# A two-layer mixed-attention block on one core: Gram products and transposed operands of the recurrence in 64x64 tiles per head

## The chip, the cores and the metric

One core of one Trainium2 chip. The metric is the device time of one execution in microseconds (us). The kernel is timed three times and the median is taken.

## The reference

Two layers work on 1280 tokens (256 of context, 1024 latent) of width 1024. Each layer projects the modulated stream once and feeds three branches: A, a bidirectional linear recurrence (6 heads x 64); B, grouped-query attention (6 query heads); C, neighbourhood attention (4 heads). They are gated, joined, projected out and normalised.

```python
def _rwkv7_step(S, inp):
    r, w, k, v, kk, b = inp
    sa = jnp.einsum('bhvk,bhk->bhv', S, kk)
    S = S * w[:, :, None, :] - sa[..., None] * b[:, :, None, :] + v[..., None] * k[:, :, None, :]
    return S, jnp.einsum('bhvk,bhk->bhv', S, r)
...
def _layer(...):
    ...
    S_f, S_b, ys_c = _rwkv_bidir(rin_c, S0, S0)
    _, _, ys_l = _rwkv_bidir(rin_l, S_f, S_b)
    ...
    y_l = jnp.concatenate([yr_l * jax.nn.silu(rg_l), ya_l * jax.nn.silu(ag_l),
                           yn_l * jax.nn.silu(ng_l)], axis=-1) @ w_out
    x = _layer_norm(DEEPNORM_ALPHA * x + gate[:, None] * y_l, ln_g, ln_b)
```

Only branch A is touched by the change. It runs over the tokens forwards and backwards, from the context into the latents.

## The kernel before, in words

A layer has four parts in the program: the input projections (matmuls into `pj`, lines 203 to 205, and their evacuations), the recurrence (`rwkv`, line 516), the attention of branches B and C (`attention`, line 831), and the output projection with the norm (lines 1144 to 1312). The code is written part after part, but a list scheduler puts the instructions of each engine in order before the kernel is built: it takes whatever it holds to be ready, the code that stands first in the program ahead of the rest. So the last projections, the recurrence and the attention are interleaved on every engine. That order is fixed when the kernel is built. On the chip each engine works through its own queue in that order and waits at its head for semaphores.

The recurrence is chunked: 32 tokens are a chunk, 128 tokens a *wave*, so that a layer has ten waves (`NW`) in each direction. The three head pairs are `c`, the direction is `d`, and the head of a pair is `p`: its 64 channels lie on partitions 64p to 64p + 63. A wave has these stages:

- `wave_pre` (line 555): loads r, kk, kd and bd, makes the decay factors (tiles `psz`, `pcu`, `lp`, `iv`) and two operand tiles: `kb` (128 partitions x 3 x 4 x 64; for each chunk 32 columns of kd and 32 of bd) and `G`. `G` has for each head `p` a block of its own. The head's own 64 partitions get kk and r (GpSimd, lines 594 and 596); the other 64 partitions are filled with zeros (GpSimd, line 593).
- `wave_gram` (line 612): for each direction `d` and each half `h` of the four chunks, six matmuls (line 620) contract `kb` with `G` over all 128 partitions into the PSUM tile `gt`. The zeros keep the two heads of a pair apart. Chunk i of the half lands on partitions 64i on. Then four VectorE instructions (line 625) multiply by the triangular mask `msk` and write into that half of `G` which held the zeros. From there on a chunk of `G` is the whole operand of a step: kk and r of the head on one half, its Gram matrix on the other.
- `wave_low` (line 600) sends a part of `G` through DRAM (`ls_d`) into `lin`. `wave_inv` (line 641) inverts small triangles from it on VectorE (lines 644 to 659), and `wave_merge` (line 673) makes the tile `tt`.
- `wave_kt` (line 628): for each `d` and `h`, three transposes of 128x128 (line 635) turn `kb` into the PSUM tile `kt`, and four ScalarE copies (line 639) put its 64x64 blocks into `S`, where the identity stands already in the other half.
- `wave_chain` (line 692): the serial part. Four steps a wave, each a chain of matmuls into `ch` (lines 713, 724, 734) with a ScalarE copy (716), four copies into `X` (730) and two VectorE products with the decay (739) between them. `out_step` (748) reads the output into `py` and copies it to `yst` (756). GpSimd clears a part of each `X` (708).

The tiles `psz`, `pcu`, `gt`, `kt`, `mg`, `py` and `pso` share one PSUM pool with two buffers (`pa`, line 523). The outer loop (line 810) runs `wave_chain(w)`, then the stages i, k, m for wave w + 2 and p, g, l for wave w + 3. `G` has six buffers, so a wave's `G` is written again three waves later.

Attention works with `sm` (scores for the row maximum, line 894, read by VectorE at line 896), `st` (scores, lines 963 and 964, read by ScalarE at line 970) and `y` (values, line 948). It waits for nothing of the recurrence, and its rows fill the engines between the stages of the waves. What is left of it when the last wave is done is worked off alone, before the output projection. [...]

Of the kernel before, what the change touches and what calls it, by code (L numbers as in the profile page):

```python
# [8 lines left out]
F32 = mybir.dt.float32  # L9
F32R = mybir.dt.float32r  # L10
AF = mybir.ActivationFunctionType
ALU = mybir.AluOpType
# [31 lines left out]
def body(tc, a):  # L44
    nc = tc.nc
# [10 lines left out]
    ident = cload("ident", [128, 128], nc.gpsimd)  # L56
    bones = cload("bones", [128, 128], nc.gpsimd)
    pp = const.tile([128, DEPTH, NPC], F32, tag="pp", name="pp")
# [457 lines left out]
    def rwkv(l, lay):  # L516
# [6 lines left out]
        pa = es.enter_context(tc.tile_pool(name=f"pa{l}", bufs=2, space=PSUM))  # L523
# [6 lines left out]
        msk = rp.tile([128, 2, 64], F32, tag="msk", name="msk")  # L530
# [24 lines left out]
        def wave_pre(w):  # L555
            dc = r2.tile([128, 2, 4, 3], F32, tag="dc", name="dc", bufs=4)
            prep[w] = dict(dc=dc, d=[], g=[])
            for d in range(2):
                t0 = 128 * wave_block(w, d)
                need_r = not (last and t0 < TC)  # L560
# [24 lines left out]
                kb = r2.tile([128, 3, 4, 64], F32, tag="kb", name="kb", bufs=2)  # L585
# [3 lines left out]
                g = G[(2 * w + d) % 6]  # L589
                for p in range(2):  # L590
                    rs_ = slice(64 * p, 64 * p + 64)
                    gv = g[rs_, :, :, p, :].rearrange("q j c f -> q c j f")
                    nc.gpsimd.memset(g[64 - 64 * p:128 - 64 * p, :, :, p, 0:64 if need_r else 32], 0.0)
                    nc.gpsimd.tensor_tensor(out=gv[:, :, :, 0:32], in0=v4(ld["kk"])[rs_], in1=lp[rs_, :, :, d:d + 32], op=ALU.mult)
                    if need_r:
                        nc.gpsimd.tensor_tensor(out=gv[:, :, :, 32:64], in0=v4(ld["r"])[rs_], in1=lp[rs_, :, :, o:o + 32], op=ALU.mult)
# [15 lines left out]
        def wave_gram(w):  # L612
            for d in range(2):
                g, kb = prep[w]["g"][d], prep[w]["d"][d][0]
                nr = prep[w]["d"][d][1]
                for h in range(2):
                    gt = pa.tile([128, 3, 2, 64], F32, tag="pp", name="gt")
                    for c in range(3):
                        for i in range(2):
                            nc.tensor.matmul(out=gt[64 * i:64 * i + 64, c, :, :nr], lhsT=kb[:, c, 2 * h + i, :], rhs=g[:, 2 * h + i, c, :, :nr],  # L620
                                             start=True, stop=True, tile_position=(0, 64 * i))
                    for i in range(2):
                        rs_ = slice(64 * i, 64 * i + 64)
                        for p in range(2):
                            nc.vector.tensor_tensor(out=g[64 - 64 * p:128 - 64 * p, 2 * h + i, :, p, :nr], in0=gt[rs_, :, p, :nr],  # L625
                                                    in1=msk[rs_, d, :nr].unsqueeze(1).to_broadcast([64, 3, nr]), op=ALU.mult)

        def wave_kt(w):
            prep[w]["s"] = S[2 * w % 4:2 * w % 4 + 2]
            for d in range(2):  # L630
                g, kb = prep[w]["s"][d], prep[w]["d"][d][0]
                for h in range(2):
                    kt = pa.tile([128, 3, 128], F32, tag="pp", name="kt")
                    for c in range(3):
                        nc.tensor.transpose(kt[:, c, :], kb[:, c, 2 * h:2 * h + 2, :].rearrange("q j f -> q (j f)"), ident)
                    for p in range(2):
                        os_ = slice(64 - 64 * p, 128 - 64 * p)
                        for j in range(2):
                            nc.scalar.copy(g[os_, 2 * h + j, :, p, :], kt[64 * j:64 * j + 64, :, 64 * p:64 * p + 64])

        def wave_inv(w):

# [776 lines left out]
```

## Time and profile before

| what | value |
|---|---|
| time, median of 3 runs | 2471.63 us (2459.14 to 2474.3) |
| the profiled execution: time / span | 2478.63 us / 2476.9 us |
| TensorE / VectorE / GpSimd / ScalarE busy share | 88% / 66% / 48% / 41% |
| mean granted TensorE clock | 0.937 |
| the chain that ended last: TensorE / VectorE / DMA / issue / ScalarE / GpSimd | 44% / 21% / 15% / 7% / 6% / 4% |
| read-out copies of the chain steps (line 716), 40 a layer: first and last start | 410.5 to 2288.8 us |

How to read it. A group's row ends in "busy us, mean ns of one", and after the next bar stands the idle time of the engine just before these instructions with what ended it. A float32 matmul leaves two records, a transpose of line 635 one; so `gt` has 960 records for 480 matmuls and `kt` 240 for 240. A matmul's duration in a row is its latency: the next one on the array starts long before it ends. What a stream of them costs is the group's busy time over its count, or the length of a burst in the timeline. "issue" is time in which the engine waited for nothing that the profile shows. PEclk is the clock that TensorE was granted.

### The profile page before, as it was taken

Reading aid. Unit: us, or ns where it says so; the run is one execution under the profiler, and the core shown is the slowest. Engines: PE = TensorE matmul, PEld = TensorE weight load, DVE = VectorE, ACT = ScalarE, POOL = GpSimd, SP = SyncE. Lnnn points to the kernel's source line nnn. Section 1 sums busy time; section 2 is a strip of 40 time slices with the busy share of each in tenths; the row PEclk is TensorE's granted clock in tenths of the full one; section 3 lists DMA queues with packets and bytes.
Section 4 is the critical chain, followed back from the end, with each engine's and each line's share of the span. In section 5 each row is a group of like instructions: output and inputs, shape, how many; then the busy total and the mean of one; then the engine's idle time right before and its main releaser. Section 6 shows DMA issues by size and latency. Waiting matters only on the chain.

```text
span 2476.9 us, 57781 instructions
## 1 busy us (share of the span) xinstructions
PE 2189.6 (88%) x22616; PEld 1645.0 (66%) x22616; DVE 1625.1 (66%) x3063; ACT 1003.5 (41%) x2186; POOL 1184.1 (48%) x1438
## 2 busy tenths in 40 slices
PE   6989999987888888989899999899868788989697
PEld 3777898765555555545897777787645555556397
DVE  5686423545768777775396785525468688778646
ACT  3333413334445454463233434223345444445522
POOL 4464426335555554462245456434456545545433
PEclk9999999996879999998999999999879999999899
DMA  7344335446555444351332445334555545332522
GB/s 281 112 162 164 111 92 123 120 108 139 126 116 136 114 100 119 102 177 34 101 103 91 146 161 182 107 90 121 141 116 140 102 99 117 84 90 64 161 71 94
DMA packets 448241, 298.17 MB, mean 120 GB/s; under 512 B 249600, under 2 KB 395880, under 8 KB 446944
## 3 DMA queue, kind: packets, MB, share of 16 engines
q1 hardware_dynamic: 439936, 281.71, 41.6%
q0 software_dynamic: 7392, 10.28, 1.5%
q8 instruction: 178, 2.92, 0.5%
q10 hardware_dynamic: 640, 2.49, 0.4%
q14 instruction: 95, 0.78, 0.1%
HBM read 198.37 MB, written 91.79 MB: 117 GB/s over the span
## 4 chain that ended last, share of the span: by engine, by line
PE 44%; DVE 21%; DMA 15%; issue 7%; ACT 6%; POOL 4%; SPq 3%; DVEq 0%; POOLq 0%; ACTq 0%
PE pj L203 5%; PE pj L204 5%; PE pj L205 5%; PE y L948 4%; DMA yf<-yg_d 3%; PE st L963 3%; PE sm L894 3%; DMA ls_d<-G 3%; DVE G L625 2%; PE st L964 2%; DVE mx L896 2%; DVE tmp L653 2%; PE ch L734 2%; PE py L754 1%; DMA lin<-ls_d 1%
## 5 line engine op out<-in xcount | busy, mean ns | idle before, releaser
L204 PE MATMUL pj<-hlo,wh 128*128 128x512 f32 (+1 forms) x1072 | 401.4, 375 | 14.3 <-DVE hlo L480 8.0
L203 PE MATMUL pj<-hhi,wh 128*128 128x512 f32 (+1 forms) x1072 | 403.2, 378 | 9.4 <-ACT qr L348 5.2
L205 PE MATMUL pj<-hhi,wl 128*128 128x512 f32 (+1 forms) x1072 | 400.6, 374 | 0.2 <-POOL wl L169 0.2
L204 PEld LDWEIGHTS pj<-hlo,wh 128*128 128x128 f32 x1072 | 205.0, 191 | 56.2 <-DVE hlo L480 8.3
L203 PEld LDWEIGHTS pj<-hhi,wh 128*128 128x128 f32 x1072 | 204.4, 191 | 54.8 <-issue 6.8
L169 POOL TENSOR_TENSOR wl<-wf,wh 128x512 fp32r<-128x512 f32 x104 | 143.8, 1387 | 202.2 <-ACT wh L168 178.7
L896 DVE TENSOR_REDUCE mx<-sm 128x1 f32<-128x512 f32 (+1 forms) x372 | 198.8, 554 | 50.1 <-PE sm L894 47.6
L205 PEld LDWEIGHTS pj<-hhi,wl 128*128 128x128 f32 x1072 | 204.9, 191 | 38.4 <-issue 3.3
L970 ACT ACTIVATE pt<-st 128x512 f32<-128x512 f32 (+1 forms) x292 | 164.9, 583 | 130.1 <-PE st L964 122.8
L948 PE MATMUL y<-pt,v 128*64 128x256 f32 (+1 forms) x1392 | 211.5, 398 | 2.3 <-ACT pt L973 1.4
L894 PE MATMUL sm<-k,q 128*128 128x256 f32 (+2 forms) x436 | 166.1, 422 | 25.8 <-DVE mx L896 19.5
L963 PE MATMUL st<-q,k 128*128 128x512 f32 (+3 forms) x376 | 165.0, 444 | 21.1 <-DVE rc L1012 5.9
L1186 PE MATMUL pj<-yh,wh 128*128 128x256 f32 x576 | 160.2, 290 | 24.4 <-ACT yh L1160 23.1
L1187 PE MATMUL pj<-yl,wh 128*128 128x256 f32 x576 | 164.0, 288 | 0.8 <-POOL yl L1161 0.8
L1188 PE MATMUL pj<-yh,wl 128*128 128x256 f32 x576 | 162.2, 286 | 0.0
L977 POOL TENSOR_TENSOR acc<-acc,pt 128x512 f32<-128x512 f32 x80 | 106.4, 1330 | 102.7 <-ACT pt L970 101.4
L948 PEld LDWEIGHTS y<-pt,v 128*64 128x64 f32 x1392 | 94.0, 142 | 89.6 <-issue 58.0
L964 PE MATMUL st<-q,k 65*128 65x512 f32 (+3 forms) x376 | 146.7, 393 | 1.9 <-ACT q L908 1.2
L894 PEld LDWEIGHTS sm<-k,q 128*128 128x128 f32 x436 | 80.6, 201 | 89.8 <-DVE mx L896 37.0
L625 DVE TENSOR_TENSOR G<-gt,msk 64x192 f32<-64x192 f32 (+1 forms) x320 | 110.5, 345 | 39.7 <-PE gt L620 28.4
L708 POOL MEMSET X<- 32x192 f32 x320 | 81.2, 254 | 102.0 <-PE py L754 74.6
L1186 PEld LDWEIGHTS pj<-yh,wh 128*128 128x128 f32 x576 | 109.9, 196 | 26.0 <-ACT yh L1160 23.5
(276 smaller groups left out, 5104.5 us busy)
## 6 DMA issues: line engine op xcount, KB each, us to landing
wf<-win SPq DMA_DIRECT2D x104, 256.0 KB
wm<-wmod SPq DMA_DIRECT2D x32, 512.0 KB
yf<-yg_d SPq DMA_DIRECT2D x72, 128.0 KB
wt<-wm SPq DMA_DIRECT2D x8, 1024.0 KB
gate_d<-o SPq DMA_DIRECT2D x32, 256.0 KB
wf<-wout SPq DMA_DIRECT2D x16, 512.0 KB
ldkk<-rw_d SPq DMA_DIRECT2D x40, 192.0 KB
ldkd<-rw_d SPq DMA_DIRECT2D x40, 192.0 KB
```

The source lines that it names most:

```text
L203: nc.tensor.matmul(out=ps[:, :n], lhsT=wh, rhs=hhi[:, k, t0:t0 + n], start=(k == 0), stop=False)
L204: nc.tensor.matmul(out=ps[:, :n], lhsT=wh, rhs=hlo[:, k, t0:t0 + n], start=False, stop=False)
L205: nc.tensor.matmul(out=ps[:, :n], lhsT=wl, rhs=hhi[:, k, t0:t0 + n], start=False, stop=(k == KT - 1))
L894: nc.tensor.matmul(out=sp_[:, :o], lhsT=q[0][:, qc:qc + 128], rhs=k[0][:, c0:c0 + o], start=True, stop=True)
L896: nc.vector.tensor_reduce(out=mx[:, n_:n_ + 1], in_=sp_[:, :o], op=ALU.max, axis=AX.X)
L948: mm = nc.tensor.matmul(out=y[64 * i:64 * i + 64, a0:a1], lhsT=v[:, t, :], rhs=pt[:, p0:p0 + a1 - a0], start=start, stop=stop and at == le ...
L963: nc.tensor.matmul(out=o, lhsT=k[0][:, 128 * t:128 * t + 128], rhs=q[0][:, qa:qb], start=True, stop=False)
L964: mm = nc.tensor.matmul(out=o, lhsT=k[1][0:65, 128 * t:128 * t + 128], rhs=q[1][0:65, qa:qb], start=False, stop=True)
L970: nc.scalar.activation(out=pt[:, :w], in_=sp_[:, :w], func=AF.Exp)
L1186: nc.tensor.matmul(out=p_, lhsT=wh[m][:, k], rhs=yh, start=(x_ == 0), stop=False)
L1187: nc.tensor.matmul(out=p_, lhsT=wh[m][:, k], rhs=yl, start=False, stop=False)
L1188: nc.tensor.matmul(out=p_, lhsT=wl[m][:, k], rhs=yh, start=False, stop=(x_ == KT - 1))
```

## The change

1. The zeros of line 593 go: 2 a wave and direction, 80 in all.
2. `wave_gram` contracts over the 64 partitions of one head at a time. For each `d` and `h` there are twelve matmuls of 64x64 by up to 64 columns instead of six of 128x64 by up to 128. Head 0 takes the array's rows 0 to 63 and columns 64 to 127, head 1 the rows 64 to 127 and columns 0 to 63, by turns. Each result lands on the partitions where `G` wants it, with both chunks of the half beside each other, and two masks of 64x384 do what four of 64x192 did.
3. `wave_kt` does the same with the identity as the moving operand: twelve matmuls of 64x64 instead of three transposes of 128x128, and two copies of 64x384 instead of four of 64x192.

Counts over the kernel: mask instructions 320 to 160, copies 320 to 160, zero fills 80 to 0, `gt` matmuls 480 to 960, `kt` 240 transposes to 960 matmuls.

```diff
@@ -590,7 +590,6 @@
                     rs_ = slice(64 * p, 64 * p + 64)
                     gv = g[rs_, :, :, p, :].rearrange("q j c f -> q c j f")
-                    nc.gpsimd.memset(g[64 - 64 * p:128 - 64 * p, :, :, p, 0:64 if need_r else 32], 0.0)
@@ -614,29 +613,34 @@
                 for h in range(2):
-                    gt = pa.tile([128, 3, 2, 64], F32, tag="pp", name="gt")
-                    for c in range(3):
-                        for i in range(2):
-                            nc.tensor.matmul(out=gt[64 * i:64 * i + 64, c, :, :nr], lhsT=kb[:, c, 2 * h + i, :], rhs=g[:, 2 * h + i, c, :, :nr],
-                                             start=True, stop=True, tile_position=(0, 64 * i))
+                    gt = pa.tile([128, 2, 3, 64], F32, tag="pp", name="gt")
                     for i in range(2):
-                        rs_ = slice(64 * i, 64 * i + 64)
-                        for p in range(2):
-                            nc.vector.tensor_tensor(out=g[64 - 64 * p:128 - 64 * p, 2 * h + i, :, p, :nr], in0=gt[rs_, :, p, :nr],
-                                                    in1=msk[rs_, d, :nr].unsqueeze(1).to_broadcast([64, 3, nr]), op=ALU.mult)
+                        for c in range(3):
+                            for p in range(2):
+                                rs_, os_ = slice(64 * p, 64 * p + 64), slice(64 - 64 * p, 128 - 64 * p)
+                                nc.tensor.matmul(out=gt[os_, i, c, :nr], lhsT=kb[rs_, c, 2 * h + i, :], rhs=g[rs_, 2 * h + i, c, p, :nr],
+                                                 start=True, stop=True, tile_position=(64 * p, 64 - 64 * p))
+                    for p in range(2):
+                        os_ = slice(64 - 64 * p, 128 - 64 * p)
+                        nc.vector.tensor_tensor(out=g[os_, 2 * h:2 * h + 2, :, p, :nr], in0=gt[os_, :, :, :nr],
+                                                in1=msk[os_, d, :nr].unsqueeze(1).unsqueeze(1).to_broadcast([64, 2, 3, nr]), op=ALU.mult)
...
-                    kt = pa.tile([128, 3, 128], F32, tag="pp", name="kt")
-                    for c in range(3):
-                        nc.tensor.transpose(kt[:, c, :], kb[:, c, 2 * h:2 * h + 2, :].rearrange("q j f -> q (j f)"), ident)
+                    kt = pa.tile([128, 2, 3, 64], F32, tag="pp", name="kt")
+                    for i in range(2):
+                        for c in range(3):
+                            for p in range(2):
+                                rs_, os_ = slice(64 * p, 64 * p + 64), slice(64 - 64 * p, 128 - 64 * p)
+                                nc.tensor.matmul(out=kt[os_, i, c, :], lhsT=kb[rs_, c, 2 * h + i, :], rhs=ident[rs_, rs_],
+                                                 start=True, stop=True, tile_position=(64 * p, 64 - 64 * p))
                     for p in range(2):
                         os_ = slice(64 - 64 * p, 128 - 64 * p)
-                        for j in range(2):
-                            nc.scalar.copy(g[os_, 2 * h + j, :, p, :], kt[64 * j:64 * j + 64, :, 64 * p:64 * p + 64])
+                        nc.scalar.copy(g[os_, 2 * h:2 * h + 2, :, p, :], kt[os_])
```

Since the scheduler orders each engine anew, rows move far from the edited lines. Lines behind the edit have numbers higher by 4 in the changed kernel. Three places follow.

TensorE in the first wave of layer 0, where the transposed operand stands beside the projections (`pj`) and the first chain step (`ch`). Before:

```order
L203 MATMUL pj<-hhi,wh 128x512
L635 MATMUL kt<-c_ident,kb 128x128 x3
L204 MATMUL pj<-hlo,wh 128x512
L205 MATMUL pj<-hhi,wl 128x512
L713 MATMUL ch<-X_2966,G_2949 32x64
L635 MATMUL kt<-c_ident,kb 128x128 x3
L713 MATMUL ch<-X_2966,G_2949 32x64
```

And in the changed kernel:

```order
L203 MATMUL pj<-hhi,wh 128x512
L639 MATMUL kt<-c_ident,kb 64x64 x24
L717 MATMUL ch<-X_2966,G_2949 32x64 x2
L717 MATMUL ch<-X_2966,G_2948 32x64 x2
L717 MATMUL ch<-X_2966,G_2949 32x64 x2
L717 MATMUL ch<-X_2966,G_2948 32x64 x2
```

Two bursts of three transposes have become one row of 24 small matmuls, two halves `h` in one go, with no projection between them.

VectorE at the masks of a later wave of layer 0, between rows of attention (`nm`, `pt`, `am`, `sm`, `acc`) and the chain's update of `X`. Before:

```order
L587 TENSOR_TENSOR kb<-ldkd,iv 128x12x32
L625 TENSOR_TENSOR G_2948<-gt,msk 64x3x64 x4
L901 TENSOR_REDUCE nm<-mx 128x1
L972 TENSOR_TENSOR pt_10837<-st,bt 128x384
L108 COPY am<-pmod 128x256
L625 TENSOR_TENSOR G_2948<-gt,msk 64x3x64 x4
```

And in the changed kernel, at the same direction of the same wave:

```order
L976 TENSOR_TENSOR pt_10972<-st,bt 128x384
L587 TENSOR_TENSOR kb<-ldkd,iv 128x12x32
L626 TENSOR_TENSOR G_2948<-gt,msk 64x6x64 x2
L905 TENSOR_REDUCE nm<-mx 128x1
L626 TENSOR_TENSOR G_2948<-gt,msk 64x6x64 x2
```

Two rows of four masks have become two rows of two, and less attention stands between them.

TensorE at the end of layer 0's recurrence: the last chain matmuls (`ch` from `S`) and the attention before them. The numbers at the names count tiles in program order; the same tile has a number higher by 400 in the changed kernel (`silu_10769` and `silu_11169` are one tile). Before:

```order
L963 MATMUL st<-q_12214,k_12206 128x512
L964 MATMUL st<-q_12215,k_9979 128x512
L894 MATMUL sm<-k_12206,q_12616 128x256
L907 MATMUL mt<-c_ident,nm 1x128
L754 MATMUL py<-X_2966,G_2948 32x64
L799 MATMUL pso<-c_ident,yo 128x128 x3
L754 MATMUL py<-X_2966,G_2948 32x64
L754 MATMUL py<-X_2966,G_2949 32x64
L894 MATMUL sm<-k_12206,q_12616 128x256
L105 MATMUL pmod<-wm,silu_10769 32x256 x4
L734 MATMUL ch<-X_2966,S_2956 64x64 x6
L734 MATMUL ch<-X_2966,S_2957 64x64 x6
```

And in the changed kernel:

```order
L952 MATMUL y<-pt_12458,v 64x128
L898 MATMUL sm<-k_11455,q_12207 128x512
L1027 MATMUL tb<-c_ident,rb 128x128 x4
L105 MATMUL pmod<-wm,silu_11169 32x256 x4
L758 MATMUL py<-X_2966,G_2948 32x64
L803 MATMUL pso<-c_ident,yo 128x128 x3
L758 MATMUL py<-X_2966,G_2948 32x64
L758 MATMUL py<-X_2966,G_2949 32x64
L898 MATMUL sm<-k_11455,q_12207 128x256
L898 MATMUL sm<-k_11455,q_12207 128x512
L738 MATMUL ch<-X_2966,S_2956 64x64 x6
L738 MATMUL ch<-X_2966,S_2957 64x64 x6
```

When the recurrence ends, the kernel before is at the keys `k_12206`, the first group of branch B. The changed one is still at the key tile before it (`k_11455`, that is 11055), the last head of branch C. Counted over the whole order, 128 of layer 0's 368 `y` matmuls stand behind the last chain row before and 172 in the changed kernel; in layer 1 it is 52 and 88 of 328.

## The prediction

> **What bounds the kernel now.** I read the page first, for the engines and for the chain of work that ended last:
>
> ```profile
> span 2476.9 us, 57781 instructions
> PE 2189.6 (88%) x22616; PEld 1645.0 (66%) x22616; DVE 1625.1 (66%) x3063; ACT 1003.5 (41%) x2186; POOL 1184.1 (48%) x1438
> PE 44%; DVE 21%; DMA 15%; issue 7%; ACT 6%; POOL 4%; SPq 3%; DVEq 0%; POOLq 0%; ACTq 0%
> ```
>
> No engine is full, and no engine has the chain to itself: it changes hands all the time. TensorE (PE) has 44% of it and VectorE (DVE) 21%. So an instruction removed counts by the share of its kind that lies on the chain, not by its whole duration.
>
> The averages mix stages, so I read the windows next. The edited lines run while the waves run. I cut each layer into the stretch of steady waves (eight of the ten) and the tail behind the last wave, where attention is alone:
>
> ```profile
> core 0: us, PE busy (x) PEld busy (x) DVE busy (x) ACT busy (x) POOL busy (x), PEclk, DMA share, GB/s
> 600.00:1055.00 455.00, 395.76 (x6237) 261.02 (x6234) 345.86 (x886) 225.20 (x570) 242.36 (x332) 0.91 0.49 118
> 1055.00:1188.00 133.00, 120.03 (x774) 68.04 (x773) 86.23 (x160) 65.03 (x127) 55.46 (x40) 0.93 0.33 99
> 1840.00:2289.00 449.00, 393.80 (x6110) 253.12 (x6111) 366.86 (x882) 224.44 (x542) 245.73 (x329) 0.95 0.43 100
> 2289.00:2345.00 56.00, 44.56 (x315) 24.12 (x313) 44.56 (x67) 34.20 (x65) 28.82 (x19) 0.95 0.45 135
> ```
>
> In the waves PE is busy 87% and 88% of the time, DVE 76% and 82%, while ScalarE (ACT) and GpSimd (POOL) are half idle. Two engines close to full, each waiting for the other in the order of its queue: that is the bound, some 57 us a wave (455 over 8).
>
> How much of the chain are the edited lines? The chain of waits by line, once for 720 us around layer 0's recurrence and once for 670 us around layer 1's:
>
> ```profile
> by line: PE y L948 4.9%; issue 4.8%; PE pj L205 4.6%; PE pj L204 4.6%; PE pj L203 4.5%; DMA ls_d<-G 4.3%; DVE G L625 4.2%; DMA X<-vt_d 3.4%; PE st L963 3.3%; PE sm L894 3.1%; ACT S L639 2.5%; DVE tmp L653 2.4%; PE ch L734 2.3%; DVE e L655 2
> by line: PE y L948 6.8%; PE sm L894 5.3%; issue 5.2%; DMA ls_d<-G 5.0%; DVE G L625 4.0%; PE pj L205 3.9%; PE st L963 3.8%; PE pj L204 3.8%; PE pj L203 3.8%; DVE tmp L653 3.2%; DVE mx L896 3.0%; PE ch L734 3.0%; PE st L964 2.9%; PE py L754 2
> ```
>
> The masks (L625) hold 4.2% of 720 and 4.0% of 670 us, 57 us together. The copies into S (L639) hold 2.5% of 720, 18 us, in layer 0; in layer 1 they stand below the last whole entry, so under 2.9%, or 19 us, and I take 10. The zero fill (L593) is in neither row.
>
> **The change part by part.** These groups give the durations:
>
> ```profile
> L625 DVE TENSOR_TENSOR G<-gt,msk 64x192 f32<-64x192 f32 x288 | 102.3, 355 | 30.8 <-PE gt L620 20.1 <-POOL G L594 4.9 <-PE ch L734 0.7
> L739 DVE TENSOR_TENSOR X<-ch,dc 64x384 f32<-64x384 f32 x156 | 86.2, 552 | 26.7 <-PE ch L734 24.9 <-PE py L754 0.3
> L639 ACT COPY S<-kt 64x192 f32<-64x192 f32 x320 | 100.1, 313 | 33.9 <-PE kt L635 20.8 <-PE ch L734 8.6
> L573 ACT ACTIVATE th<-psz 128x384 f32<-128x384 f32 x40 | 19.8, 494 | 2.7 <-PE psz L571 2.4
> L593 POOL MEMSET G<- 64x768 f32 x72 | 53.2, 739 | 35.1 <-PE py L754 25.4 <-PE ch L713 3.5 <-issue 3.0
> L620 PE MATMUL gt<-G,kb 128*64 128x128 f32 x864 | 63.3, 292 | 5.9 <-ACT iv L583 3.0 <-POOL kb L588 2.8
> L635 PE MATMUL kt<-c_ident,kb 128*128 128x128 f32 x240 | 44.8, 300 | 10.4 <-DVE tt L689 7.3 <-ACT S L639 3.2
> L734 PE MATMUL ch<-X,S 128*64 128x64 f32 x1920 | 87.3, 242 | 11.0 <-DVE X L730 10.4 <-issue 0.6
> L724 PE MATMUL ch<-rsb,tt 32*32 32x64 f32 x1920 | 47.4, 229 | 2.1 <-ACT rsb L716 2.0
> ```
>
> *Masks.* 288 take 355 ns for 192 columns. A product of the new size, 64x384 out of PSUM with a broadcast operand, is L739: 552 ns. 144 of these make 79.5 us instead of 102.3, 22% less (the 32 narrower masks go the same way). Of the 57 us on the chain, 22% is **13 us gained**. Bounds: nothing, if DVE waits for PE anyway; 25 us, if DVE is the bound throughout. What is late next is the way of `G` through DRAM (`ls_d`, 4.3% and 5.0% of the chain): it starts earlier by what the masks save and is as long as before.
>
> *Copies.* 320 of 313 ns against 160 of some 494 ns (L573, 384 columns out of PSUM): 100.1 to 79.0 us, 21% less. Of 28 us on the chain that is **6 us gained**; bounds 0 and 21.
>
> *Zero fill.* 53.2 us of POOL and a little more for the eight narrower ones. I take **nothing**. The fill's idle time, 25.4 us for `py`, is the wait until the old `G` has been read, and the products behind it (L594, L596) write the same tile: they inherit that wait. The cover is POOL's half idle time in the waves. A gain is bounded by 5 us: 53 of POOL's 1184 us, that share of the 4% (99 us) that POOL has on the chain. A loss has no way in, since nothing else is put on that queue.
>
> *TensorE.* Here the change adds. The lengths of bursts, from the timeline:
>
> ```profile
> 653.74 0.38 PE L996 MATMUL ls<-acc,onec 128*32 128x256 f32 x1
> 654.27 0.49 PE L635 MATMUL kt<-c_ident,kb 128*128 128x128 f32 x3
> 657.89 0.55 PE L635 MATMUL kt<-c_ident,kb 128*128 128x128 f32 x3
> 676.62 0.88 PE L620 MATMUL gt<-G,kb 128*64 128x128 f32 x12 [1.66 <-POOL kb L588]
> 553.56 0.92 PE L734 MATMUL ch<-X,S 128*64 128x64 f32 x24 [2.57 <-DVE X L730]
> ```
>
> Both new bursts are twelve matmuls, 24 records, of 64 weight columns and 64 moving columns in two tiles by turns. That is L734's burst but for the rows of the array: 0.92 us. `gt` took 0.88 us, `kt` 0.55. There are 80 bursts of each kind (2 layers, 10 waves, 2 directions, 2 halves): +0.04 x 80 = 3 us and +0.37 x 80 = 30 us of PE. By the groups' means the new `kt` would cost 87.3 instead of 44.8 us, +42. PE's idle eighth may hide some of it; I count PE's share of the chain, 44% of 33: **14 us lost**. Bounds: 0, if attention waits for other things, and 45.
>
> That needs the two tiles to run side by side although they use different rows of the array and write one PSUM bank. L724 does just that with four tiles: 47.4 us for 1920 records is 25 ns each, against 45 ns for L734's two. The Trainium skill says the opposite under "TensorEngine Tiling (Array Packing)", in "Gotcha 1: PSUM Pressure": different row tiles cannot access the same PSUM bank at once. By that rule the pairs would run one after the other; by L724 they do not. I go by the row, and the rule is the last rival below.
>
> *The order.* The scheduler has put the attention later. Behind layer 0's last chain row stand 172 of the `y` matmuls instead of 128, in layer 1 88 instead of 52. What that weighs, from the windows of line 948 alone, which count two records a matmul, and from one window of the projections:
>
> ```profile
> 600.00:1055.00 455.00, 73.33 (x472) 32.76 (x472) 0.91 0.49 118
> 1055.00:1188.00 133.00, 37.57 (x256) 17.05 (x256) 0.93 0.33 99
> 1840.00:2289.00 449.00, 82.08 (x536) 35.63 (x536) 0.95 0.43 100
> 2289.00:2345.00 56.00, 16.68 (x120) 7.53 (x120) 0.95 0.45 135
> ...
> 0.00:360.00 360.00, 324.60 (x1676) 264.81 (x1677) 213.58 (x190) 123.85 (x201) 159.68 (x156) 0.99 0.47 156
> ```
>
> In the tails one `y` and all that goes with it takes 133/128 = 1.04 and 56/60 = 0.93 us. So the tails grow by 44 x 1.04 + 36 x 0.93 = 80 us. Against it, the recurrence starts earlier: 64 and 52 fewer projection matmuls stand ahead of the second wave, at 0.19 us (324.60 over 1676 records): 22 us. And the waves have 80 fewer `y` among them. If DVE sets their pace, these give back what DVE spends on them, 86.23/128 = 0.67 us each, 54 us. Net: 80 - 22 - 54 = **4 us lost**. The ends are wide: all 80 given back (PE is as full in the waves as in the tail) is a gain of 22; nothing given back is a loss of 58.
>
> *Sum.* -13 - 6 + 14 + 4 = -1 us on the profiled execution's 2478.6. The median of the three runs is 7 us under that execution, so I forecast **2470 us: no change that can be measured**. The three runs span 0.6%; less than 1% either way (25 us) cannot be told from none.
>
> **The rivals.**
>
> *A: DVE is the bound and PE's extra work disappears.* Then all 25 us of the masks count, the copies' 6 and GpSimd's 5, PE's 33 us lie in its idle eighth, and the order comes out even: -36 us, 2436. For it: DVE busy 76% to 82%, and the masks are the dearest DVE line on the chain. Against it: PE holds twice DVE's share.
>
> *B, slower: the attention is pushed out and not paid back.* The waves have a floor made of waits from engine to engine, and the attention in them rode along free. For it, the two layers compared: layer 1 puts 268 `y` into its steady waves and takes 449 us, layer 0 only 236 and takes 455. (Layer 1 does less for the context, so this overstates.) Then +58 from the order, -19 + 14 from the edits: +53, about 2524; with half of the 54 us paid back, 2497. The point from which it decides: 80 less 22 over 16 waves, that is, the waves must fall from 57 us to under 53.4, or the time is lost.
>
> *C: the tiles do not run side by side.* Each of 3840 records then costs up to 45 ns more (L734's rate for a pair, halved): 175 us of PE, 44% of it on the chain, +77, about 2547. Against it stands L724. This is what the skill's rule would give.
>
> *D: the masks do not get shorter*, because the wait for `gt`, 20.1 us of L625's idle time, grows instead. That leaves +12, inside the forecast.
>
> **How the numbers follow.** Forecast with D 0.39, A 0.34, B 0.22, C and the unnamed 0.05. Faster by over 1%: A, 0.34. Within 1%: 0.39. Slower: B and C, 0.27. The range takes in A's 2436 with 6 us below it, and B with half or less of its price unpaid: 2430 to 2515. Beyond lie B's far end and C, and a few hundredths below A.
>
> **What would show it.** Right: 144 masks near 550 ns and 160 copies near 490; `kt` bursts of 24 records in 0.9 us; PE some 30 us busier; tails of about 180 and 90 us; steady waves of 53 us. The forecast is wrong towards A if the waves fall under 51 us, wrong towards B if they stay over 55, and the step on the tiles is wrong if a burst of 24 takes over 1.3 us at full clock.

## The result and the profile after

| | before | changed | ratio [95% interval] |
|---|---|---|---|
| median of 4 runs each | 2468.15 us | 2552.89 us | 1.0348 [1.0301, 1.0395] |
| profiled execution, span | 2476.9 us | 2550.9 us | |

The changed kernel is slower by 85 us, outside the range and on the side of rival B. Ratios and intervals, here and below, are of the fast runs: they leave out one execution of e6 (3347 us) and two of e16 (2960 and 9538 us). The page's head, as before:

```profile
span 2550.9 us, 62681 instructions
PE 2259.9 (89%) x25256; PEld 1709.2 (67%) x25256; DVE 1597.3 (63%) x2903; ACT 979.5 (38%) x2026; POOL 1132.9 (44%) x1358
```

Every engine but TensorE has less to do, and the whole still takes longer. The groups of the edited lines (by form for the masks):

```profile
L626 DVE TENSOR_TENSOR G<-gt,msk 64x384 f32<-64x384 f32 x144 | 79.9, 555 | 25.6 <-PE gt L622 22.2
```

```profile
L639 PE MATMUL kt<-c_ident,kb 64*64 64x64 f32 x1920 | 78.6, 232 | 12.7 <-DVE tt L693 11.7 <-ACT S L643 1.0
L643 ACT COPY S<-kt 64x384 f32<-64x384 f32 x160 | 75.8, 473 | 45.3 <-PE kt L639 39.1 <-PE ch L738 3.9
L622 PE MATMUL gt<-G,kb 64*64 64x64 f32 (+1 forms) x1920 | 70.5, 229 | 3.6 <-POOL lp L581 2.0 <-POOL kb L588 1.6
```

and four bursts of one wave, from the timeline:

```profile
650.05 0.92 PE L639 MATMUL kt<-c_ident,kb 64*64 64x64 f32 x24
651.57 0.91 PE L639 MATMUL kt<-c_ident,kb 64*64 64x64 f32 x24
664.83 0.92 PE L622 MATMUL gt<-G,kb 64*64 64x64 f32 x24 [0.46 <-POOL kb L588]
666.74 0.92 PE L622 MATMUL gt<-G,kb 64*64 64x64 f32 x24
```

So the local prices came out: masks 555 ns (552 expected), copies 473 (494), bursts 0.92 us (0.92). TensorE as a whole is busy 70 us longer, where some 30 were expected; the groups `kt` (44.8 to 78.6) and `gt` (67.8 to 70.5) make 37 of that. Most of the time is lost elsewhere. The windows of the same stages as before (steady waves and tail of each layer):

```profile
core 0: us, PE busy (x) PEld busy (x) DVE busy (x) ACT busy (x) POOL busy (x), PEclk, DMA share, GB/s
593.40:1037.90 444.50, 373.01 (x6757) 256.88 (x6758) 307.71 (x785) 202.56 (x484) 217.24 (x296) 0.86 0.50 119
1037.90:1211.00 173.10, 161.41 (x1078) 90.42 (x1078) 123.05 (x221) 85.09 (x170) 75.45 (x54) 0.99 0.33 97
1885.50:2334.50 449.00, 398.12 (x6747) 263.51 (x6746) 329.13 (x783) 203.14 (x465) 217.40 (x297) 0.89 0.41 98
2334.50:2424.00 89.50, 78.45 (x485) 43.16 (x484) 66.62 (x105) 49.57 (x93) 47.23 (x31) 0.92 0.30 90
```

The tails grew from 133 and 56 to 173 and 90 us, as the prediction had it. The waves did not give it back: 445 and 449 us after 455 and 449, with PE and DVE less busy in layer 0 and a lower granted clock in both (0.86 and 0.89 after 0.91 and 0.95). A third place is the start of layer 1, from the first to the third wave's read-out copy; the windows of before and of the changed kernel:

```profile
1672.00:1840.00 168.00, 138.77 (x1733) 108.65 (x1732) 88.92 (x250) 60.02 (x149) 71.92 (x103) 0.86 0.53 128
```

```profile
1694.30:1885.50 191.20, 150.42 (x2184) 119.76 (x2183) 91.06 (x239) 58.45 (x129) 67.83 (x98) 0.87 0.50 118
```

The chain of waits by line around layer 1's recurrence, 670 us as before:

```profile
by line: PE y L952 9.9%; PE sm L898 6.4%; PE st L967 5.6%; PE pj L1190 4.4%; issue 4.3%; PE st L968 4.3%; PE pj L1191 4.3%; PE pj L1192 4.2%; DMA ls_d<-G 3.8%; PE kt L639 3.1%; PE ch L738 2.8%; PE py L758 2.8%; DVE mx L900 2.4%; DVE tmp L65
```

The masks, 4.0% before, are no longer among the first lines. `y` rose from 6.8% to 9.9% of the chain, and the transposed operand's matmuls came in with 3.1%.

By stages, the ends of which are read-out copies (lines 716 and 720), the 74 us between the two spans are:

| stage | changed less before, us |
|---|---|
| up to layer 0's third wave | -6.5 |
| steady waves, layer 0 | -10.1 |
| last chain step of layer 0 to the first of layer 1 | +38.9 |
| start of layer 1 (two waves) | +23.2 |
| steady waves, layer 1 | +0.2 |
| last chain step of layer 1 to the end | +28.3 |

Executions of the kernel before ranged from 2459 to 2474 us here and from 2456 to 2487 us over all comparisons, so a single entry under some 10 us says little.

### The profile page after: what moved, and what is told of

Read it like the earlier page. It is cut to its first block, busy times and chain, and to the rows that moved or that the text cites. A ratio compares the mean times of both kernels' runs of the same rounds, so it can differ in the third digit from the quotient of the medians.

```text
span 2550.9 us, 62681 instructions
## 1 busy us (share of the span) xinstructions
PE 2259.9 (89%) x25256; PEld 1709.2 (67%) x25256; DVE 1597.3 (63%) x2903; ACT 979.5 (38%) x2026; POOL 1132.9 (44%) x1358
## 5 line engine op out<-in xcount | busy, mean ns | idle before, releaser
L900 DVE TENSOR_REDUCE mx<-sm 128x1 f32<-128x512 f32 (+1 forms) x372 | 198.4, 552 | 43.2 <-PE sm L898 41.7
L981 DVE TENSOR_TENSOR acc<-acc,pt 128x512 f32<-128x512 f32 x112 | 102.2, 921 | 41.6 <-ACT pt L974 41.2
```

The lines of the kernel that those rows point to most:

```text
L900: nc.vector.tensor_reduce(out=mx[:, n_:n_ + 1], in_=sp_[:, :o], op=ALU.max, axis=AX.X)
L981: eng.tensor_tensor(out=acc[i][:, :w], in0=sums[i][:, :w], in1=pt[:, :w], op=ALU.add)
```

## The experiments

Two theories to begin with. **O**: the loss is the place of attention, which stands later on TensorE (172 and 88 `y` behind the last chain rows instead of 128 and 52). **I**: place is of no matter, the edited instructions' own time decides. All 18 runs at a glance (difference of the median to that of the kernel before in the same comparison; the third column counts the `y` behind the last chain rows):

| run | us | `y` behind | ratio [95% interval] |
|---|---|---|---|
| e1 changed, attention ahead | +82 | 128, 64 | 1.0309 [1.0258, 1.0359] |
| e2 before, attention held back | +19 | 160, 92 | 1.0079 [1.0056, 1.0103] |
| e3 Gram half alone | +42 | 136, 80 | 1.0166 [1.0128, 1.0204] |
| e4 transposed-operand half alone | +39 | 171, 79 | 1.0156 [1.0118, 1.0195] |
| e5 changed, before's TensorE interleave | +57 | 128, 52 | 1.0235 [1.0189, 1.0281] |
| e6 before, changed TensorE interleave | +57 | 172, 80 | 1.0229 [1.0183, 1.0276] |
| e7 Gram half, zeros kept | +54 | 128, 64 | 1.0211 [1.0162, 1.0261] |
| e8 Gram half over 128 rows | +19 | 128, 64 | 1.0076 [1.0040, 1.0112] |
| e9 before, bare waves | +307 | 368, 328 | 1.1241 [1.1181, 1.1302] |
| e10 changed, bare waves | +354 | 368, 328 | 1.1430 [1.1372, 1.1488] |
| e11 Gram half, before's interleave | +39 | 124, 52 | 1.0157 [1.0111, 1.0203] |
| e12 transposed half, before's interleave | +50 | 124, 52 | 1.0187 [1.0141, 1.0232] |
| e13 Gram half, bare waves | +342 | 368, 328 | 1.1382 [1.1319, 1.1445] |
| e14 transposed half, bare waves | +292 | 368, 328 | 1.1180 [1.1120, 1.1241] |
| e15 as e8, bare waves | +336 | 368, 328 | 1.1359 [1.1296, 1.1421] |
| e16 as e8, before's interleave | +10 | 124, 52 | 1.0039 [1.0016, 1.0062] |
| e17 changed, masks ahead of the inverse | +50 | 172, 80 | 1.0204 [1.0177, 1.0231] |
| e18 as e17, before's interleave | +52 | 128, 52 | 1.0210 [1.0181, 1.0239] |

**e1 and e2: the fill put back, and taken away.** e1 schedules the changed kernel's attention with a higher priority; e2 holds the attention of the kernel before until chain step 10 of a layer (`follow` orders two instructions on one engine without a semaphore).

```diff
-        attention(l)
+        with tc.high_priority(offset=(2900, 2450)[l]):
+            attention(l)
```

```diff
+                steps.append(mm)
...
+        late = [steps[40 * l + (10, 10)[l]]]
...
+                        if late:
+                            follow(mm, late.pop())
```

> The changed kernel with all its edits; only the scheduler's priority of attention is raised (2900 instructions earlier in layer 0, 2450 in layer 1), so that 128 and 64 value matmuls stand behind the layers' last chain rows, where the kernel before has 128 and 52 and the changed kernel 172 and 88. Theory O (the order): the chain's waves have a floor, and attention inside them is free. Tails fall back to about 133 and 67 us, the steady waves stay near 445 and 449 us: 2553 - 41 - 22 = 2490 us. Theory I (the added instructions): the longer bursts of TensorE hold up the chain, the place of the attention does not matter, since moved work takes its time with it: 2553 us, steady waves longer by what the tails lose.

> The kernel before with all its instructions; only the first score matmul of each layer's attention is tied behind the chain's step 10, so that 160 and 92 value matmuls stand behind the last chain rows instead of 128 and 52. Theory O: the tails grow by 32 and 40 us and the waves shorten by little: 2468 + 60 to 72 = 2528 to 2540 us. Theory I: nothing is added, so 2468 us within 1%.

Measured: +82 and +19 us. e1 came out as theory I had it (2554 us for 2553). Against the changed kernel the stages behind the last chain steps shrank by 38 and 19 us, and the steady waves grew by 48 and 18, to 492 and 467: attention that had missed the first waves came in the last ones, at up to 45 `y` a wave, and made these up to 71 us long. So attention in the waves is not free by itself. e2 is within the 1% that theory I allows, yet its loss is clear of zero; it is under a third of what theory O asked for.

**e3 and e4: one half of the change each.** e3 has the new `wave_gram` without zeros and the old `wave_kt`; e4 the old `wave_gram` with zeros and the new `wave_kt`.

> The Gram half of the change alone (no zeros, 64x64 Gram matmuls, two masks); the transposes and four copies stay. 136 and 80 value matmuls behind the last chain rows. Theory O: tails 8 and 28 us longer than before, less some us for the shorter masks: about 2495 us. Theory I: the Gram bursts are as long as before (0.91 against 0.88 us), so all of the gain and none of the loss: 2450 to 2468 us.

> The other half alone (twelve 64x64 matmuls for three transposes, two copies for four); zeros, Gram matmuls and four masks as before. 171 and 79 value matmuls behind the last chain rows. Theory O: tails 43 and 27 us longer: about 2535 us, as bad as nearly the whole change. Theory I: 30 us of TensorE added at 44% or in full: 2480 to 2500 us.

Measured: +42 and +39: e3 at 2515 us is above both theories' numbers, e4 at 2512 between them. They add up to the whole, which speaks against a conflict between the halves, but each scheduled attention anew, so code and order are still mixed.

**e5 and e6: code and order apart.** Here each chain step's first matmul is tied, both ways, to the exact counts of `y` and of score matmuls that stood ahead of it in the other kernel. Only these two kinds of matmuls on TensorE are tied; the scheduler orders the rest, and the other engines, anew. No run ties the kernel before to its own counts, so what the ties cost by themselves is not known; e16 below, with these ties, is 10 us over before.

```diff
+        for k in range(40 * l, 40 * l + 40):
+            for done, n in zip((ym, sc), AHEAD[k]):
+                if n > BASE[l][done is sc]:
+                    follow(steps[k], done[n - 1])
+                if n < len(done):
+                    follow(done[n], steps[k])
```

> The changed kernel's instructions, TensorE's interleave pinned to that of before: each chain step has exactly as many `y` and score matmuls ahead of it as in the kernel before (128 and 52 `y` behind the last chain rows, not 172 and 88). Theory O (the loss is the order of attention against the waves): 2470, as before. Theory I (the loss is in the new instructions, wherever attention stands): 2553, nothing comes back. Mixed, from the run with 72 `y` pushed out for +18 us, 0.26 us each: 84 `y` brought back are 21 us, so 2532.

> The kernel before's instructions (full-height Gram matmuls, transposes, four masks, four copies, zeros), TensorE's interleave pinned to that of the changed kernel (172 and 80 `y` behind the last chain rows). Theory O: 2550. Theory I: 2470. Mixed at 0.26 us per `y` for 72 `y`: 2490, as in the run where attention was held back.

Measured: +57 each. e5 is near the mixed case (2529 us for 2532). e6 lies between theory O and the mixed case, nearer to O (2528 for 2550 and 2490), and it is the main result: not one instruction of the change is in it, and the place of attention alone, with the order that the other engines get from it, costs 57 us. Its steady waves fell as little as those of the changed kernel, at the same lower clock:

```profile
592.40:1033.10 440.70, 357.38 (x5967) 245.20 (x5968) 318.51 (x835) 206.71 (x537) 224.19 (x324) 0.88 0.47 113
1856.40:2308.70 452.30, 383.65 (x5959) 250.08 (x5961) 343.75 (x835) 212.90 (x516) 234.88 (x321) 0.90 0.41 98
```

By the stages of the table above e6 stands at -7.5, -13.9, +43.2, -5.4, +3.5 and +25.8 against before. The changed kernel differs from e6 by less than 5 us in every stage but one: the start of layer 1, +28.6. So at the changed kernel's order the loss of 74 us by the profiles splits into 46 for the order and 28 for the code, all of it at that one place.

e5 taken alone would say that the code costs as much again. But pinning brought in a wait of its own. The longest waits of TensorE around its second wave:

```profile
engine line waited for: us in total, times, longest us
PE sm L905 <- POOL q L886: 32.5, 1, 32.5
PE psz L574 <- DMA zs<-zs_d: 2.1, 1, 2.1
```

The first score matmul stands where before's order wants it, but GpSimd, whose order was not pinned, makes its `q` later. Over the whole of e5 this wait is 35.4 us, in e11 14.6, in e12 18.8, in e18 36.0, in e16 0.2, in the changed kernel 6.9, and in e6 and the kernel before 1.8. Not all of it is lost time: up to layer 0's third wave, where its longest piece lies, e5 is 22 us behind before, and e16, which does not have it, some 10. Behind that, by the stages of the table above, e5 stands at +23.3, -16.3, +15.1, +5.1 and +0.8. So by the profiles the new code costs between 28 us at the old order, if the wait made all of the first 22, and 50. With e6's 46 that is 74 to 95 us, and the whole change costs 74: order and code add up in the first case alone, which is not shown. What differs most is the steady waves of layer 0, where the new code costs 23 us at the old order and nothing clear of noise at the new one.

**e7 and e8: the tiles of 64 rows.** e7 puts the zero fill back into e3, e8 contracts over all 128 rows as well, with the same twelve matmuls, columns and two masks (its loop over `c` stands outside that over `i`, as in the kernel before; in e7 it is the other way round):

```diff
-                                nc.tensor.matmul(out=gt[os_, i, c, :nr], lhsT=kb[rs_, c, 2 * h + i, :], rhs=g[rs_, 2 * h + i, c, p, :nr],
-                                                 start=True, stop=True, tile_position=(64 * p, 64 - 64 * p))
+                                nc.tensor.matmul(out=gt[os_, i, c, :nr], lhsT=kb[:, c, 2 * h + i, :], rhs=g[:, 2 * h + i, c, p, :nr],
+                                                 start=True, stop=True, tile_position=(0, 64 - 64 * p))
```

> The Gram half alone as in e3 (64x64 tiles, two masks, old transposes and four copies), with the zero fill of G put back: only GpSimd has more to do. The scheduler then stands 128 and 64 `y` behind the last chain rows, not 136 and 80. Theory O: 24 `y` fewer at 0.26 us, 2508, or by the whole loss being order, some 2482. Theory T (tiles of 64 rows slow TensorE itself, by drains at each switch and a lower clock): 2508 to 2515, as e3.

> As e7, same order (128 and 64), same two masks, same 12 matmuls per group and same columns, but each over all 128 rows with the zeros of G, so no row tiles, only the two column tiles that before has too. Theory T (64-row tiles): the loss goes, 2455 to 2475. Theory N (it is the number of matmuls, or the faster masks releasing work earlier, not the row tiles): as e7, 2505 to 2515.

Measured: +54 and +19. Keeping the zeros gained nothing although 24 fewer `y` stand behind the last rows than in e3, so theory O alone does not explain the Gram half. Full-height tiles are 34 us cheaper than tiles of 64 rows (by two thirds of the loss, theory T). The height is not all that differs, though: beside the order of the loop, attention lies otherwise within the waves (layer 0's second and third wave hold 4 and 26 `y` in e7, none and 19 in e8). And e8's masks, half as many, still brought no gain over before.

**e9 and e10: waves without attention.** The line of e2 with step 39 of each layer in place of 10.

> The kernel before, all attention of a layer held on TensorE until the last chain step's matmuls (368 and 328 `y` behind them). It shows what a wave takes by itself. Theory W (a wave waits for itself: its own chain of engines sets its length, attention fills the holes): the 31 steps from the third wave on keep most of their 455 and 449 us, some 400 each, at a low clock. Theory P (TensorE's work sets the length): they fall by the time of the 323 and 377 thousand columns taken out at the tails' 0.7 to 0.9 us per thousand, to about 200 each. Whole time: W 2900, P 2500.

> The same with the changed kernel's instructions; the order of attention is now one and the same. Theory L (a wave of the new code is longer by itself, as the first lightly filled wave of the changed kernel and of the transposed-operand half was, 62 to 68 us beside 50): the 31 steps take 60 to 100 us per layer more than in e9. Theory C (only the clock or the order differ under attention): within 10 us of e9, or shorter by the faster masks and copies.

Measured: +307 and +354. The steady waves (31 chain steps a layer) of e9 and of e10:

```profile
596.20:937.80 341.60, 217.86 (x4786) 174.28 (x4786) 178.95 (x484) 115.07 (x347) 139.84 (x260) 0.63 0.37 87
1986.10:2313.80 327.70, 212.68 (x4776) 169.38 (x4776) 171.55 (x469) 108.09 (x329) 129.07 (x245) 0.64 0.35 82
```

```profile
592.10:949.10 357.00, 231.28 (x5576) 189.62 (x5577) 167.50 (x436) 109.92 (x296) 129.28 (x234) 0.64 0.39 92
2010.00:2356.10 346.10, 223.74 (x5568) 183.03 (x5569) 158.17 (x422) 100.21 (x281) 113.60 (x223) 0.67 0.33 76
```

For e9 between the two, nearer to W: a wave keeps three quarters of its length with no attention in it, while PE is busy 64% and DVE 52% of the time at a clock of 0.63. No engine is near full, which leaves the waves' own round of waits between engines and transfers to set the rest. 240 and 276 `y` left the waves, which fell by 113 and 121 us, 0.47 and 0.44 us each. From the last chain step to the next layer or the end it took 264 and 276 us more, 1.10 and 1.00 each. That is the price of pushing attention out: about 1.05 paid, 0.45 given back. By it, e6's 44 + 28 `y` cost 44 x 1.10 + 28 x 1.00 - 72 x 0.45 = 44 us, and its profile shows 46. By stages that is partly luck: 69 us were paid behind the last chain steps for 76, 10 given back in the steady waves for 32, and 13 came from the stages ahead of them, which the price does not know. For the 40 `y` more that e2 has behind layer 1 and 32 behind layer 0 it would give 43, and e2 lost 19: there layer 1's third wave had no attention at all and took 44 us, so which waves go empty matters too.

The same can be read wave by wave. Mean length of the third to eighth waves, by the `y` that they hold (before, e2, e6 and e9 for the old code; the changed kernel, e1, e5, e10, e17 and e18 for the new; number of waves in brackets):

```
y in the wave   0          2 to 9    15 to 24   25 to 29   30 to 37   38 to 49
old code, us    46.0 (13)  50.0 (2)  59.9 (4)   61.7 (12)  60.5 (14)  65.4 (3)
new code, us    49.6 (12)  63.5 (3)  58.4 (12)  60.6 (21)  63.4 (15)  68.3 (9)
```

Between 15 and 37 `y` a wave of the old code takes 60 us, however many there are. Thinning the fill in that range gives nothing back.

e10 over e9 is the new code at one and the same place of attention: 15 and 18 us in the steady waves and 18 at the start of layer 1, neither theory L's 60 to 100 a layer nor theory C's 10. Under attention the first two do not show at the new order (the changed kernel over e6: +4 and -3); at the old one layer 0's does (e5: +23, e11: +25, e12: +21, e18: +29).

**e11 and e12: the halves at before's interleave.**

> The Gram half alone (64x64 tiles, two masks, no zeros), TensorE's interleave pinned to before's. Theory I (the loss of e3 is in the instructions): 2505 to 2515. Theory O: 2470. With the order priced by e6, 57 us for 72 `y`, the 32 `y` that e3 stood further behind are 25 us, so 2490.

> The transposed-operand half alone (64x64 matmuls for the transposes, two copies), TensorE's interleave pinned to before's. Theory I: 2512, as e4. Theory O: 2470, since e4 stood 70 `y` further behind and e6 paid 57 us for 72. If the two halves add up at before's order to the 57 us of e5, e11 and e12 stand together 57 us over before.

Measured: +39 and +50, with the pin's own wait of 14.6 and 18.8 us in them. At 2507 us e11 is where theory I had it, and e12 at 2518 is 6 us above theory I's number; theory O's 2470 is out for both. Each half costs as much at before's order as at its own (e3 +42, e4 +39). They stand 89 over before together, not 57, so the halves are not additive here. The pin's wait lies ahead of layer 0's third wave, and there e11 is 3 us ahead of before and e12 11 behind. Behind it, e11 and e12 lose 25 and 21 us in layer 0's steady waves and 11 and 12 at the start of layer 1.

**e13 to e15: which half lengthens the bare wave.**

> The Gram half alone, attention held behind the last chain step as in e9. If the bare wave is lengthened by bursts of TensorE that stand in the steps' way (theory B), the Gram half costs nothing here, since its bursts last as long as before's and its masks are shorter: 31 steps within 6 us of e9's 342 and 328, whole time 2765 to 2780. If 64-row tiles slow TensorE beside the bursts (theory T): 10 to 20 us per layer more, 2800 to 2815.

> The transposed-operand half alone, attention held as in e9. Theory B: all the loss of e10 is here, 357 and 346 us, whole time 2815 to 2825. Theory T: half of it or less, 2790 to 2800.

> As e13, with the Gram matmuls over all 128 rows and the zeros of G kept (the code of e8). Theory B: as e13 within 6 us a layer. Theory T: 10 to 20 us a layer under e13, at e9 or below it.

Measured in the steady waves, for e13, e14 and e15 in turn:

```profile
588.10:958.60 370.50, 222.09 (x5075) 177.35 (x5075) 173.38 (x436) 117.31 (x349) 126.95 (x233) 0.64 0.37 87
1999.30:2351.00 351.70, 219.64 (x5064) 176.13 (x5065) 163.39 (x422) 107.54 (x330) 113.97 (x223) 0.65 0.32 76
```

```profile
588.50:929.50 341.00, 221.46 (x5295) 179.73 (x5289) 179.44 (x484) 108.68 (x295) 143.61 (x260) 0.70 0.40 93
1982.10:2301.80 319.70, 213.85 (x5280) 173.88 (x5280) 167.59 (x470) 100.22 (x280) 127.53 (x244) 0.72 0.36 84
```

```profile
590.60:954.90 364.30, 221.83 (x5074) 177.62 (x5074) 167.38 (x436) 116.28 (x347) 140.88 (x252) 0.63 0.37 86
1994.80:2342.40 347.60, 216.29 (x5064) 172.56 (x5065) 163.25 (x422) 107.85 (x330) 128.35 (x243) 0.65 0.33 76
```

The opposite of theory B: the half with the longer bursts (e14) costs nothing in bare waves, the half with bursts as long as before's and shorter masks (e13) costs 29 and 24 us. Nor is it the 64-row tiles: e15, over 128 rows, costs 23 and 20. So the Gram half lengthens a wave from 46 to 51 us by something that no duration of its own instructions accounts for. e14 costs nothing only in sum: its third wave in layer 0 is as long as e13's (62 and 61 us, 45 in e9), and the five after it are shorter than e9's. Weight loads of the merge `mg`, the step between the inverse and the chain, show where TensorE waits more. The wait for VectorE's `di` in layer 1's steady waves, of e9, e13 and e14:

```profile
PEld mg L684 <- DVE di L687: 10.2, 3, 5.5
```

```profile
PEld mg L685 <- DVE di L688: 28.9, 5, 6.6
```

```profile
PEld mg L687 <- DVE di L690: 20.9, 6, 5.9
```

In e13's TensorE queue the second merge stands a third of a chain step earlier than in e9, and the chain's matmuls queue behind it. e14 has a good part of that wait and is not longer, so this is a reading, not a proof; it was not tried alone. At the start of layer 1 it is the transposed-operand half that costs more: 167 us in e9, 175 in e13, 182 in e14, 185 in e10.

**e16: full-height Gram tiles at before's interleave.**

> The code of e8 (full-height Gram matmuls, two masks) with TensorE's interleave pinned to before's. If the 39 us of e11 come from the 64-row tiles: 2465 to 2475, and with masks of 555 ns for two of 355 perhaps under before. If they come from the scheduler's old order not fitting the new code's masks: 2500 to 2510, as e11.

Measured: +10 us, nearest to the first case and still not under before. It is the best of all versions with new code, 29 us under e11, and no version beat the kernel before. The wait of e11's pin does not explain that: ahead of layer 0's third wave, where it lies, e16 is 13 us behind e11, and in layer 0's steady waves it is 32 us shorter (448 us for 480). The two differ in the height of the tiles, the zeros and the order of the loop.

**e17 and e18: VectorE's queue.** The trace of e15 showed a candidate for the Gram half. Before the change the copy that begins the inverse (`nn`, line 644) mostly stands behind all sixteen masks of its wave. In the changed kernel it stands ahead of the last two or four of eight, in 14 of 20 waves, and it waits for a transfer (`lin`). e17 orders it behind the last mask; e18 pins TensorE to before's interleave too.

```diff
+                        prep[w]["m"] = nc.vector.tensor_tensor(out=g[os_, 2 * h:2 * h + 2, :, p, :nr], in0=gt[os_, :, :, :nr],
...
+            follow(n0, prep[w]["m"])
```

> The changed kernel with one thing more: the copy that begins the inverse of a wave is ordered on VectorE behind the last of the wave's eight masks. TensorE's interleave stays (172 and 80 `y` behind the last chain rows, not 172 and 88). Theory V (the copy, which waits for a transfer, holds up masks behind it on VectorE): the 29 and 24 us that the Gram half cost the bare waves come back as far as attention does not hide them; by the 39 us of e11, 2505 to 2520. Theory N (VectorE's order is of no matter): 2550.

> The same order on VectorE in the changed kernel, and TensorE's interleave pinned to before's (128 and 52 `y` behind). Theory V: e5's 2528 less some 39 to 53 us, 2475 to 2490, and level with before or below it if nothing else of the loss is in the instructions. Theory N: 2528, as e5.

Measured: +50 and +52. e17 is 34 us under the changed kernel by the differences to before, 32 by the profiles, and so near theory V's number (2528 us for 2505 to 2520). But its steady waves barely moved:

```profile
587.40:1029.10 441.70, 370.66 (x6757) 253.94 (x6758) 306.10 (x785) 202.46 (x484) 216.09 (x296) 0.88 0.50 120
1867.20:2312.50 445.30, 393.58 (x6771) 261.29 (x6770) 332.41 (x792) 205.23 (x469) 220.06 (x301) 0.91 0.42 99
```

They are 3 and 4 us shorter; 11 us of the gain lie behind layer 1's last chain step, where 80 `y` stand instead of 88, and the rest is spread over all stages. e18 is no better than e5 (+52 for +57), although at this order there was a loss in layer 0's steady waves to win back (+29 over before, e5 +23). So under attention theory V does not hold as the cause: the masks' place on VectorE is worth a few us in the waves at most. In bare waves, where the 29 and 24 us were seen, it was not tried.

## Why the prediction was wrong

- **Masks and copies.** Durations right, gain not seen. The 13 us of the masks were their share of the chain times 22%. e8 and e16 have those masks with full-height tiles and are 19 and 10 us over before, not under it; but they also have twice the Gram matmuls, and no run has the masks or the copies alone. That a wave whose round of waits has other members does not shorten by what one member saves is the reading that fits.
- **TensorE.** Bursts right to a hundredth of a microsecond, and tiles that use different rows and the same bank do run side by side: 24 records in 0.92 us, as L734's pairs over all rows. So rival C is out, and that its 2547 us lies nearest to the measured 2553 is chance. The Trainium skill says in "TensorEngine Tiling (Array Packing)", "Gotcha 1: PSUM Pressure", that row tiles cannot access one bank at once; the bursts here, in which they write different partitions of one bank in 0.92 us, disagree, and the measurement decides.
- **The order: the step that failed.** "These give back what DVE spends on them, 0.67 us each, 54 us." The tails' 80 us came about nearly as predicted: 74 by the windows. The waves gave back 10 us in the changed kernel and 10 in e6, where only the order is new. DVE does not set the pace of the waves: empty, with DVE busy half of the time, they still take 46 us (e9), and between 15 and 37 `y` their length does not depend on the fill. The average given back is 0.45 us a `y`, not 0.67, and near the actual fill less. The price of the order was +4 in the sum and is 46 us in e6's profile, 57 by its medians.
- **The earlier start.** -22 in the sum. Measured: -6 us up to layer 0's third wave, but +23 at the start of layer 1. e6 has -5 there, so it is the new code: in the bare waves the transposed-operand half brings 15 and the Gram half 8 of it, both together 18. PE is busy 12 us longer there, 7 of them in the new `kt` matmuls (15.5 us after 8.4) and 6 in projections. Of the other 11 us the trace shows where TensorE stands idle: it waits 6.7 us for GpSimd's `q` ahead of a score matmul, and 11.7 instead of 5.3 us for VectorE's `tt` ahead of `kt`. e10 is nearly as slow there (185 us) without the first of these waits, so the cause is open.
- **Rival B** named the mechanism ("a floor made of waits from engine to engine, and the attention in them rode along free") and the point from which it decides, waves over 53.4 us; they took 55.6 and 56.1. (Both figures divide windows of 31 steps by eight waves of four; a whole wave took 57.4 and 57.9 us, 58.7 and 57.9 before, which moves the point as well and decides the same.) Its far end, 2524 us, is 29 short of the measured time; the start of layer 1, where the changed kernel stands 28.6 us over e6, is in no rival. It was underrated at 0.22, because TensorE's 87% in the waves was read as a bound. e9 shows that much of that business is fill. Quite free the fill is not: a `y` taken out gives back 0.45 us.

Still open: why the Gram half with 64-row tiles is 34 us dearer than with full-height ones under attention (e7, e8) and 6 in bare waves (e13, e15), what in the Gram half lengthens the bare wave, why the new code lengthens layer 0's steady waves at the old order and not at the new one, and what it does at the start of layer 1.

## What to carry to other kernels

Before costing a change in a loop that other work fills, ask what the loop takes with the fill held out: if it is far above the engines' busy time, fill is cheap inside and dear behind, and what an edit does to the *place* of the fill outweighs its durations. An edit that changes durations makes a list scheduler move everything; tie the old interleave to the new code, and the new one to the old code, to see what each does without the other, and look at the pinned run, stage by stage, for waits that the pin itself makes. The two prices need not add up. A duration times its share of the chain is no sure gain where the chain is a round of waits over several engines.

## What was not expected of the hardware

- The clock that TensorE is granted follows the fill: 0.91 and 0.95 in the filled waves before, 0.86 and 0.89 in the changed kernel, 0.88 and 0.90 in e6, 0.63 and 0.64 with attention held out. In e9's bare waves the chain's own matmuls (`ch`) are busy 102 and 100 us, with the same records 78 and 73 before, so the lower clock may be one reason why these waves give so little back. In the changed kernel's it is not: 80 and 72 us. The Trainium skill says in "TensorE: Matmul & The Clock Gate", "What's actually happening", that the default is throttled and activity releases it; the rows agree, with 0.91 and 0.95 under the fill and 0.63 and 0.64 without it.
- The transposed operand made by matmuls instead of transposes left the clock higher: 0.70 and 0.72 in e14's bare waves after 0.63 and 0.64 in e9's, with PE busy nearly as long (221 and 214 us after 218 and 213). In e10, which has the new Gram matmuls too, it is 0.64 and 0.67.
